# A seven-product second MLP layer whose GpSimd work is handed to VectorE, ScalarE and adding transfers

## The chip, the cores and the metric

The kernel runs on one core of one Trainium2 chip. The metric is the device time of one execution in microseconds (us). Five engines matter: TensorE (PE in the profile, with PEld for its weight loads), VectorE (DVE), ScalarE (ACT), GpSimd (POOL) and the sync engine (SP), which only issues transfers. A transfer can be issued from the queue of SP, of ScalarE or of GpSimd.

## The reference, cut to what matters

One decoder layer on 512 tokens of width 1024. Four branches (sparse attention, gated linear attention, RG-LRU, HGRN2) are merged by gates and projected; then comes the MLP that the change is about:

```python
merged = (gates[:, :, 0] * (y_a @ w_br_a[l]) + gates[:, :, 1] * (y_b @ w_br_b[l])
          + gates[:, :, 2] * (y_c @ w_br_c[l]) + gates[:, :, 3] * (y_d @ w_br_d[l]))
x = x + merged @ w_out[l]
h2 = rms_norm(x, norm2_g[l])
x = x + jnp.square(jax.nn.relu(h2 @ w_ff1[l])) @ w_ff2[l]
return rms_norm(x, final_norm_g)
```

`w_ff1` is 1024x4096 and `w_ff2` 4096x1024, all float32.

## The kernel before

Every matmul operand is split into a high part (a cast to float32r, on ScalarE, L209 for weights) and a low part (operand minus high part, L211, on VectorE, or on GpSimd for weight units 5 to 23). `mm3` (L223 to L229) then issues three matmuls: high by high, high by low, low by high. A weight unit is loaded by SP into a raw buffer, and `split` cuts it into two pieces; the pool `whl` holds four pieces of high and four of low parts.

The stages follow one another on TensorE: input projections with the four branches between them, the gates (32 steps: four branches in the order 2, 0, 3, 1 by eight column blocks `m`, each adding into `merged[m]` on GpSimd, L1052), the output projection, the first MLP layer (`ff1`, 32 units) and the second MLP layer.

The second layer is a 2x2 block product of the hidden activations by `w_ff2`, done in seven products instead of eight (`PRODS`). Product `n` names a left operand (a hidden block `H`, or the difference of two), a right operand (a block of `w_ff2`, or a sum or difference of two, kept in DRAM as `right[...]`) and the output quadrants `(i, j)` into which it is added with a sign. Products 0, 1, 2, 5 and 6 have a difference on the left; products 3 and 4 have a plain block. Each product runs over eight units `g` of twelve matmuls (two pieces by two output strips `t` by three), into two PSUM banks.

What feeds a unit, and what the change touches:
- `make_left(n, g)` makes the left operand: where there is a difference, GpSimd subtracts into a `q` tile (L1195); ScalarE casts the high part (L1204); the low part (L1205) is made by VectorE, or by GpSimd where there was no difference. It is called one product ahead, at the same unit. For product 0 it is called during ff1. `behind` adds ordering without a semaphore; the order on each engine is otherwise set by a planner from the priorities of the bands (`BANDS`: evictions, then weight splits, ..., then `left`, then `mm`).
- `right_unit` loads and splits the right operand, one load on SP and two casts and two subtractions per unit.
- After a product, each of its output strips is evicted by VectorE, `xt += r2 * psum` (L1328): 24 of them, eight of which are the last for their tile `xt[tt, j]` and are followed by a square on ScalarE and, when a row is complete, by `row_out` (final norm and store).
- The right operands that are sums are made in DRAM in 16 pieces of 1 MB: `begin_sum` copies the first block (issued from ScalarE's queue, L1019) and `add_sum` adds the second with an accumulating transfer (issued from GpSimd's queue, L1024). The one that is a difference is made by `difference` (two loads, a GpSimd subtraction L1221, a store L1222) in 16 pieces, during ff1.
- The `q`, `da`, `db`, `sq` and `out` tiles share the tag `y` of NY = 8 buffers. Left operands take twelve places in turn.

## Time and profile before

| | us |
|---|---|
| median of 3 runs | 910.13 |
| lowest, highest | 908.9, 910.93 |
| the profiled execution | 908.9 |
| its span in the trace | 907.1 |
| PE busy | 854.0 (94%) |
| DVE busy | 623.8 (69%) |
| ACT busy | 455.0 (50%) |
| POOL busy | 363.5 (40%) |

Busy time of PE is time with some matmul in flight; a matmul of 512 columns is recorded with 0.39 us but the next one starts before it ends. A row of a timeline gives the start, the length from the first start to the last end, the engine, the line, the operation and how many of them were merged into the row. A row by stretch gives the busy time and the count of instructions of each engine, then the granted clock of TensorE as a share of full speed, the mean busy share of the 16 DMA engines and what they moved.

### The profile page before, as it was taken

What the parts mean: (1) busy time and instruction counts of PE and PEld (TensorE: products, weight loads), DVE (VectorE), ACT (ScalarE), POOL (GpSimd) and SP (SyncE); (2) the same over time, 40 slices, a digit from 0 to 9 for tenths busy, and PEclk for the clock granted to TensorE, in tenths of its full rate; (3) what the DMA queues carried; (4) which work ended last, traced back from release to release, by engine and by line L of the source; (5) the groups of instructions that cost most, each with busy time, mean ns of one, the idle gap of its engine ahead of it and who ended that gap; (6) DMA issues with size and microseconds to landing.
All of it is one profiled execution on the core that took longest, in us unless ns stands there. A gap on an engine that the chain in (4) does not pass through costs nothing.

```text
span 907.1 us, 11859 instructions
## 1 busy us (share of the span) xinstructions
PE 854.0 (94%) x4206; PEld 676.1 (75%) x4206; DVE 623.8 (69%) x1038; ACT 455.0 (50%) x789; POOL 363.5 (40%) x313
## 2 busy tenths in 40 slices
PE   8979978999899999999999999999999969998995
PEld 7757866767677667678888888888888846886674
DVE  8896999797866497966334553434444499769994
ACT  7428664355745673455333443433333345665563
POOL 6345865552432174524222222232222293357500
PEclk9989998999999989999999999999999999999998
DMA  6223212212223245234853598799999646664552
GB/s 242 94 96 105 94 47 87 64 53 76 71 99 110 77 151 186 99 106 164 288 185 106 152 243 202 206 262 270 256 263 258 220 158 196 193 195 140 160 175 83
DMA packets 39083, 141.31 MB, mean 156 GB/s; under 512 B 4683, under 2 KB 6128, under 8 KB 38768
## 3 DMA queue, kind: packets, MB, share of 16 engines
q1 hardware_dynamic: 32880, 102.80, 33.5%
q0 software_dynamic: 5632, 20.97, 11.2%
q10 hardware_dynamic: 512, 16.78, 5.2%
q8 instruction: 33, 0.54, 0.2%
q14 instruction: 26, 0.21, 0.1%
HBM read 134.24 MB, written 40.64 MB: 193 GB/s over the span
## 4 chain that ended last, share of the span: by engine, by line
PE 67%; DVE 23%; issue 4%; ACT 3%; DMA 1%; POOL 1%; SPq 0%; DVEq 0%; POOLq 0%; ACTq 0%
PE m_f L226 6%; PE m_f L225 6%; PE m_f L227 6%; DVE lo L211 6%; PE m_gt L227 5%; PE m_gt L225 5%; PE m_gt L226 5%; PE m_g L226 3%; PE m_g L227 3%; PE m_g L225 3%; PE m_o L225 2%; PE m_o L226 2%; PE m_o L227 2%; PE dal L236 1%; DVE sc L564 1%
## 5 line engine op out<-in xcount | busy, mean ns | idle before, releaser
L209 ACT CAST hi<-raw 128x512 fp32r<-128x512 f32 (+2 forms) x198 | 127.2, 649 | 193.9 <-PE m_f L226 68.2
L211 DVE TENSOR_TENSOR lo<-raw,hi 128x512 fp32r<-128x512 f32 (+2 forms) x160 | 133.3, 837 | 130.7 <-ACT hi L209 128.7
L211 DVE TENSOR_TENSOR lo<-w,hi 128x512 fp32r<-128x512 f32 x112 | 104.0, 947 | 25.8 <-ACT hi L209 25.2
L209 ACT CAST hi<-w 128x512 fp32r<-128x512 f32 x112 | 69.5, 622 | 72.2 <-PE m_g L227 56.7
L227 PE MATMUL m_gt<-hh,lo 128*128 128x512 f32 x256 | 101.5, 397 | 0.0
L226 PE MATMUL m_gt<-hh,hi 128*128 128x512 f32 x256 | 101.5, 396 | 0.0
L225 PE MATMUL m_gt<-hh,hi 128*128 128x512 f32 x256 | 100.8, 394 | 0.0
L225 PE MATMUL m_f<-fh,hi 128*128 128x512 f32 x256 | 99.8, 390 | 0.0
L227 PE MATMUL m_f<-fh,lo 128*128 128x512 f32 x256 | 99.7, 390 | 0.0
L226 PE MATMUL m_f<-fh,hi 128*128 128x512 f32 x256 | 99.6, 390 | 0.0
L1195 POOL TENSOR_TENSOR q<-hd,hd 128x512 f32<-128x512 f32 x40 | 63.5, 1602 | 80.1 <-DVE hd L1237 63.9
L211 POOL TENSOR_TENSOR lo<-raw,hi 128x512 fp32r<-128x512 f32 (+1 forms) x38 | 59.6, 1574 | 45.6 <-ACT hi L209 41.6
L1052 POOL TENSOR_TENSOR mg<-mg,gt 128x512 f32<-128x512 f32 x24 | 41.2, 1719 | 80.5 <-DVE gt L1051 80.5
L226 PEld LDWEIGHTS m_gt<-hh,hi 128*128 128x128 f32 x256 | 48.3, 189 | 11.8 <-issue 1.5
L225 PEld LDWEIGHTS m_gt<-hh,hi 128*128 128x128 f32 x256 | 48.3, 189 | 11.1 <-issue 1.1
L227 PEld LDWEIGHTS m_gt<-hh,lo 128*128 128x128 f32 x256 | 48.2, 188 | 10.9 <-issue 0.3
L227 PEld LDWEIGHTS m_f<-fh,lo 128*128 128x128 f32 x256 | 48.1, 188 | 10.0
L225 PEld LDWEIGHTS m_f<-fh,hi 128*128 128x128 f32 x256 | 48.1, 188 | 9.9
L226 PEld LDWEIGHTS m_f<-fh,hi 128*128 128x128 f32 x256 | 48.1, 188 | 9.8
L1221 POOL TENSOR_TENSOR da<-da,db 128x512 f32<-128x512 f32 x16 | 21.6, 1350 | 63.9 <-DMA db<-in_wts_dram 57.9
L1041 ACT ACTIVATE gt<-m_gt,hbg 128x512 f32<-128x512 f32 x32 | 22.0, 686 | 32.6 <-PE m_gt L227 32.4
L1051 DVE SCALAR_TENSOR_TENSOR gt<-gt,m_br 128x512 f32<-128x512 f32 x24 | 16.4, 684 | 27.0 <-PE m_br L227 26.9
(868 smaller groups left out, 2064.5 us busy)
## 6 DMA issues: line engine op xcount, KB each, us to landing
raw<-in_wts_dram SPq DMA_DIRECT2D x62, 512.0 KB, 4.4
raw<-in_wts_dram SPq DMA_DIRECT2D x32, 640.0 KB, 4.0
w<-right SPq DMA_DIRECT2D x40, 512.0 KB, 4.2
right<-in_wts_dram POOLq DMA_DIRECT2D x16, 1024.0 KB, 9.9
w<-in_wts_dram SPq DMA_DIRECT2D x16, 512.0 KB, 3.5
da<-in_wts_dram SPq DMA_DIRECT2D x16, 256.0 KB, 5.3
db<-in_wts_dram SPq DMA_DIRECT2D x16, 256.0 KB
right<-da POOLq DMA_DIRECT2D x16, 256.0 KB, 9.9
```

Of the source, the lines that this page charges most:

```text
L209: stream["copy"] = S.copy(hi[:, c], raw[:, rc])
L211: stream["lo"] = eng.tensor_sub(lo[:, c], raw[:, rc], hi[:, c].bitcast(F32))
L225: mms = [P.matmul(out, lh, rh, start=start, stop=False), P.matmul(out, lh, rl, start=False, stop=False), P.matmul(out, ll, rh, start=False ...
L226: P.matmul(out, lh, rl, start=False, stop=False),
L227: P.matmul(out, ll, rh, start=False, stop=stop)]
L236: i = P.matmul(*a, **k)
L564: V.match_replace(sc[:, :nk], m8, sc[:, :nk], SENT)
L1041: i_gate[:] = [S.activation(gt, ps, AF.Tanh, scale=0.5, bias=hbg[:, n * 8 + m:n * 8 + m + 1])]
L1051: V.scalar_tensor_tensor(gt, gt, 1.0, ps, op0=OP.add, op1=OP.mult)
L1052: G.tensor_add(merged[m], merged[m], gt)
L1195: G.tensor_sub(t, H[plus, g], H[minus, g])
L1221: i_sub = G.tensor_sub(a, a, b)
```

## The change

- `make_left` is cut into `prepare_left` (the difference, now on VectorE) and `split_left` (the cast on ScalarE and the low part, now always on VectorE). Both run along the units counted through all products: at unit `q` the difference for unit `q + 8` is made, and the split for unit `q + AHEAD`, AHEAD = 6. They are ordered behind the last cast and the last low part of the unit's right operand.
- An eviction that is not the last for its tile is made by ScalarE into a `y` tile (`o`), and an accumulating transfer issued from GpSimd's queue adds it to `xt`. That is 16 of the 24 evictions; the eight last ones stay on VectorE.
- The copies of `begin_sum` are issued at gate steps 2 to 17 (of 32) instead of at two of three steps from 8 on. Eight of the 16 `add_sum` are issued in the last two gate branches (every second step from 16), four stay in the output projection and four are left in ff1, where there were twelve.
- The last 18 matmuls of the last product are held in the written order, which puts the last nine of strip 0 ahead of the last nine of strip 1.

```diff
--- before.py
+++ after.py
@@ -28,6 +28,7 @@
 LEVELS = (32, 16, 8, 4, 2, 1)
 TCARGS = {"schedule_with_timeline_sim": True}
 NPM_BANKS, NA_BANKS, NG_BANKS = 3, 3, 2
+AHEAD = 6
 LAG = 3
 PIECES = 2
 LO0, LO1 = 5, 24
@@ -60,6 +61,9 @@
     ((0, 0), (1, 1), "11-22", ((1, 1, 1), (0, 0, 1))),
     ((0, 1), (1, 1), "21+22", ((0, 0, 1),)),
 )
+
+
+GATES = (2, 0, 3, 1)
 
 
 def gate_units(n):
@@ -1026,7 +1030,6 @@
     merged = [yp.tile([128, T], F32, tag="mg", bufs=KT, name=f"mg{m}") for m in range(KT)]
 
     i_gate = []
-    begun = {"n": 0}
 
     def gates(n, is_first, last):
 
@@ -1035,9 +1038,9 @@
             ps, hi, lo = std_tile(("gate", n, m), f"gt{n}{m}", hh, hl)
             with band("ev"):
                 gt = yp.tile([128, T], F32, tag="gt", bufs=NG, name=f"gt{n}{m}")
-                if not is_first and m % 3 < 2 and begun["n"] < len(pieces):
-                    begin_sum(begun["n"], i_gate)
-                    begun["n"] += 1
+                step = GATES.index(n) * KT + m
+                if 2 <= step < 2 + len(pieces):
+                    begin_sum(step - 2, i_gate or [stream["copy"]])
                 i_gate[:] = [S.activation(gt, ps, AF.Tanh, scale=0.5, bias=hbg[:, n * 8 + m:n * 8 + m + 1])]
             yh, yl = SH[n]
             with band("mm"):
@@ -1049,7 +1052,9 @@
                     V.scalar_tensor_tensor(merged[m], gt, 1.0, ps, op0=OP.add, op1=OP.mult)
                 else:
                     V.scalar_tensor_tensor(gt, gt, 1.0, ps, op0=OP.add, op1=OP.mult)
-                    G.tensor_add(merged[m], merged[m], gt)
+                    i_add = G.tensor_add(merged[m], merged[m], gt)
+                    if step >= 16 and step % 2 == 0:
+                        add_sum((step - 16) // 2, [i_add])
                 if last is not None:
                     dump(f"mg{m}", merged[m])
                     h, l = last(f"mgh{m}", FR), last(f"mgl{m}", FR)
@@ -1151,7 +1156,7 @@
                 S.activation(sq, x2[m], AF.Square)
                 i_acc = G.tensor_add(acc, acc, sq)
                 if m % 2:
-                    add_sum(m // 2, [i_acc])
+                    add_sum(8 + m // 2, [i_acc])
 
 
     xt, r2 = {}, {}
@@ -1185,14 +1190,20 @@
     turns = {"left": 0, "raw": 0}
     H, left = {}, {}
 
-    def make_left(n, g, after=None):
+    def prepare_left(n, g, after=()):
 
         plus, minus = PRODS[n][0:2]
+        t = H[plus, g]
+        if minus is not None:
+            with band("left"):
+                t = yy(f"q{n}{g}")
+                behind([V.tensor_sub(t, H[plus, g], H[minus, g])], after[1:])
+        left[n, g] = t
+
+    def split_left(n, g, after=()):
+
+        t = left[n, g]
         with band("left"):
-            t = H[plus, g]
-            if minus is not None:
-                t = yy(f"q{n}{g}")
-                G.tensor_sub(t, H[plus, g], H[minus, g])
             k = turns["left"] % 12
             turns["left"] += 1
             if k < 8:
@@ -1201,12 +1212,8 @@
             else:
                 h = persist.tile([128, 2, T], FR, tag=f"p{k - 8}", name=f"l{n}{g}")
                 h, l = h[:, 0], h[:, 1]
-            i_h = S.copy(h, t)
-            i_l = (V if minus is not None else G).tensor_sub(l, t, h.bitcast(F32))
-            if after:
-                behind([i_h], after[:1])
-                if minus is not None:
-                    behind([i_l], after[1:])
+            behind([S.copy(h, t)], after[:1])
+            behind([V.tensor_sub(l, t, h.bitcast(F32))], after[1:])
             left[n, g] = h, l
 
     def difference(c):
@@ -1239,11 +1246,12 @@
             if n == 2:
                 turn()
         if j == 1 and kk == 1:
-            make_left(0, g)
+            prepare_left(0, g)
+            split_left(0, g)
         if n % 2 and n // 2 < 16:
             i_sub = difference(n // 2)
-            if n // 2 < 12:
-                add_sum(4 + n // 2, [i_sub])
+            if n // 2 < 4:
+                add_sum(12 + n // 2, [i_sub])
     with band("ev"):
         i_ln = S.preload_act_table_set("natural_log_exp_and_others")
         behind([i_ln], i_gate)
@@ -1301,7 +1309,7 @@
                 SY.dma_start(gf, bass.AP(tensor=gf_in.tensor, offset=gf_in.offset, ap=[[0, 128], [1, D]]))
         with band("mm"):
             pss = [(mbank if n % 2 else abank)(f"m_g{n}{t}") for t in range(2)]
-        blocks = {}
+        blocks, mms = {}, []
 
         order = [(k, t) for k in range(16) for t in range(2)]
         if n == len(PRODS) - 1:
@@ -1313,21 +1321,31 @@
                 for kk in range(2):
                     c = slice(kk * 256, (kk + 1) * 256)
                     blocks[k + kk] = lh[:, c], ll[:, c], hi[kk], lo[kk]
-                if n + 1 < len(PRODS):
-                    make_left(n + 1, k // 2, [stream["copy"], stream["lo"]])
+
+                after = [stream["copy"], stream["lo"]]
+                q = n * 8 + k // 2
+                if q + 8 < len(PRODS) * 8:
+                    prepare_left(*divmod(q + 8, 8), after)
+                if 8 <= q + AHEAD < len(PRODS) * 8:
+                    split_left(*divmod(q + AHEAD, 8), after)
             with band("mm"):
                 lh_, ll_, hi_, lo_ = blocks[k]
                 c = slice(t * 128, (t + 1) * 128)
-                mm3(pss[t], lh_[:, c], ll_[:, c], hi_, lo_, k == 0, k == 15)
+                mms += mm3(pss[t], lh_[:, c], ll_[:, c], hi_, lo_, k == 0, k == 15)
+        if n == len(PRODS) - 1:
+            in_line(mms[-6 * LAG:])
         for i, j, sign in outs:
             todo[i, j] -= 1
         for t in range(2):
             for i, j, sign in outs:
                 tt = 2 * i + t
                 with band("ev"):
+                    if todo[i, j]:
+                        o = yy(f"o{n}{tt}{j}")
+                        S.activation(o, pss[t], AF.Copy, scale=r2[tt, sign])
+                        G.dma_start(xt[tt, j], o, accum_op=OP.add)
+                        continue
                     V.scalar_tensor_tensor(xt[tt, j], pss[t], r2[tt, sign], xt[tt, j], op0=OP.mult, op1=OP.add)
-                    if todo[i, j]:
-                        continue
                     S.activation(yy(f"sq{tt}{j}"), xt[tt, j], AF.Square, accum_out=ssq[:, 2 * tt + j:2 * tt + j + 1])
                     if (i, j) == (0, 1):
                         pre[tt] = {1: yy(f"pre{tt}")}
```

## Rows read from the trace of the kernel before

**Rows 1.** By stretch: busy us (x count) by engine, granted clock, DMA share, GB/s

```profile
160.00:320.00 160.00, 153.74 (x896) 113.87 (x895) 114.62 (x272) 89.52 (x164) 56.82 (x58) 1.00 0.23 78
320.00:400.00 80.00, 76.89 (x492) 59.07 (x490) 64.84 (x105) 41.52 (x64) 43.34 (x41) 0.96 0.42 145
400.00:500.00 100.00, 100.00 (x461) 81.70 (x460) 47.97 (x65) 45.17 (x65) 28.65 (x17) 1.00 0.50 175
500.00:722.00 222.00, 222.00 (x1000) 184.24 (x999) 97.97 (x170) 83.29 (x145) 61.60 (x61) 1.00 0.85 233
722.00:765.00 43.00, 32.98 (x134) 23.94 (x133) 42.14 (x40) 20.67 (x36) 30.04 (x19) 1.00 0.51 174
765.00:822.00 57.00, 57.00 (x253) 47.13 (x252) 42.16 (x54) 36.57 (x62) 21.85 (x16) 1.00 0.65 202
822.00:866.00 44.00, 37.85 (x153) 27.45 (x152) 44.00 (x45) 25.35 (x48) 29.16 (x18) 1.00 0.46 143
866.00:897.00 31.00, 31.00 (x138) 25.54 (x136) 23.09 (x45) 15.68 (x30) 0.00 (x0) 1.00 0.41 136
```

**Rows 2.** Waits from 720 us on: waiter, releaser: total us, times, longest

```profile
PE m_g L226 <- DVE lo L211: 15.9, 13, 2.3
```

**Rows 3.** Timeline of GpSimd in the second layer

```profile
724.08 14.82 POOL L1195 TENSOR_TENSOR q<-hd,hd 128x512 f32<-128x512 f32 x9 [9.63 <-DVE hd L1237]
...
749.09 0.56 POOL L1222 DMA_DIRECT2D right<-da  x1
...
825.69 13.57 POOL L1195 TENSOR_TENSOR q<-hd,hd 128x512 f32<-128x512 f32 x8
```

**Rows 4.** Timeline of VectorE in the second layer: beside GpSimd, and without

```profile
732.64 1.74 DVE L211 TENSOR_TENSOR lo<-w,hi 128x512 fp32r<-128x512 f32 x1
...
761.10 0.68 DVE L1205 TENSOR_TENSOR l21l<-q,l21h 128x512 fp32r<-128x512 f32 x1
...
761.70 1.28 DVE L211 TENSOR_TENSOR lo<-w,hi 128x512 fp32r<-128x512 f32 x2
...
791.74 1.04 DVE L211 TENSOR_TENSOR lo<-w,hi 128x512 fp32r<-128x512 f32 x1 [0.67 <-ACT hi L209]
...
794.46 1.04 DVE L211 TENSOR_TENSOR lo<-w,hi 128x512 fp32r<-128x512 f32 x1 [0.67 <-ACT hi L209]
```

**Rows 5.** Timeline: first matmul of product 0; evictions after products 3 and 6

```profile
722.00 0.39 PE L225 MATMUL m_g<-hi,l00h 128*128 128x512 f32 x1
...
822.29 2.72 DVE L1328 SCALAR_TENSOR_TENSOR xt<-m_g,r,xt 128x512 f32<-128x512 f32 x4
...
896.87 1.41 DVE L1328 SCALAR_TENSOR_TENSOR xt<-m_g,r,xt 128x512 f32<-128x512 f32 x2 [3.68 <-PE m_g L227]
```

**Rows 6.** Timeline of the tail

```profile
896.90 0.39 PE L227 MATMUL m_g<-hi,l67l 128*128 128x512 f32 x1
...
899.77 0.75 DVE L1289 SCALAR_TENSOR_TENSOR out<-xt,fv,gf 128x512 f32<-128x512 f32 x1
...
900.39 0.61 ACT L1331 ACTIVATE sq<-xt 128x512 f32<-128x512 f32 x1
...
902.49 0.75 DVE L1289 SCALAR_TENSOR_TENSOR out<-xt,fv,gf 128x512 f32<-128x512 f32 x1
```

**Rows 7.** Groups of ScalarE, from the page: count, busy us, mean ns

```profile
L209 ACT CAST hi<-w 128x512 fp32r<-128x512 f32 x112 | 69.5, 622 | 72.2 <-PE m_g L227 56.7
...
L1041 ACT ACTIVATE gt<-m_gt,hbg 128x512 f32<-128x512 f32 x32 | 22.0, 686 | 32.6 <-PE m_gt L227 32.4
```

**Rows 8.** Transfers: the queue of GpSimd (page); landing of line 1222 (its own answer)

```profile
q0 software_dynamic: 5632, 20.97, 11.2%
...
DMA to landing us min/median/max: 2.6/9.9/16.0
```

**Rows 9.** Issues by line, of the tensor `right`: ns min/median/max, first and last start

```profile
L1019 ACTq DMA_DIRECT2D right<-in_wts_dram x16: 496/496/604, 241.5 to 471.5; - x16
...
L1024 POOL DMA_DIRECT2D right<-in_wts_dram x16: 860/894/1135, 514.2 to 689.3; - x16
```


## The prediction

> **What bounds the kernel now.** I read the stretches first [rows 1]. From 400 to 722 us TensorE is busy without a gap, 322 of 322 us, so nothing that is added or taken away beside it there moves the end unless it stops TensorE. From 722 us, where the second MLP layer starts, the picture changes twice. In 722 to 765 and in 822 to 866 TensorE is busy for 32.98 of 43 and 37.85 of 44 us, while VectorE is full (42.14 and 44.00 us) and GpSimd is busy for 30 and 29 us. In 765 to 822 and 866 to 897 TensorE is full again and VectorE has room. The waits say who is late: TensorE's low-by-high matmul waits for VectorE's low parts [rows 2]. The granted clock is 1.00 in all of these rows, which is the upper of the two levels, so the clock has no part in it.
>
> The timelines say why VectorE is late. The two stretches are those in which GpSimd makes `q` differences one after another, nine in 14.82 us from 724.08 and eight in 13.57 us from 825.69 [rows 3]. Beside them one low part takes VectorE 1.74 us; without GpSimd the same subtraction takes 0.68, and in a series one starts every 0.60 us (761.10 to 761.70; two in 1.28) [rows 4]. So it isn't the count of VectorE's instructions that stops TensorE but that two engines, each reading two operands, take turns. `make_left` is called at each unit, but nothing holds the GpSimd part back, so the differences of a product bunch at its start.
>
> **The gain at hand.** In the undisturbed part, low parts at the same place of two successive units start at 791.74 and 794.46 [rows 4]: 2.72 us per unit of twelve matmuls. Product 0 starts at 722.00, the evictions after product 3 at 822.29, those after product 6 at 896.87 [rows 5]. Products 0 to 3 took 100.29 us for 32 units that need 32 x 2.72 = 87.04, so 13.25 us are lost; products 4 to 6 took 74.58 us for 24 x 2.72 = 65.28, so 9.30 are lost. Together 22.5 us.
>
> **Part 1, differences to VectorE.** What it removes: the slow turns, and with them the 22.5 us, if VectorE can carry the work. What it adds: per unit VectorE then has two low parts of the right operand, one low part of the left and, for products whose successor has a difference, one difference: 4 x 0.60 = 2.40 us of 2.72 (products 0, 1, 4 and 5), 3 x 0.60 = 1.80 in products 2 and 3, two in most of product 6. It fits, with 0.3 us to spare per unit where it is fullest. It holds only while a subtraction takes 0.60; at 0.68 (its recorded length, were none overlapped with the next) four take 2.72 and nothing is to spare. I take 0.60, since series of that kind stand in the trace. What is queued behind a difference on VectorE is the next unit's low part; it is delayed by at most a difference and a left low part, 1.2 us, while four pieces of right operand are buffered (4 x 1.36 = 5.44 us of matmuls). The GpSimd low parts of products 3 and 4 also move to VectorE; they are counted in the three and four. In ff1 the eight differences of product 0 move too; VectorE is busy for 97.97 of 222 us in 500 to 722 [rows 1], so they cost nothing. One `difference` subtraction and two small products for the final norm stay on GpSimd: at most three times about 1.1 us of delay on VectorE, covered by the same buffer.
>
> **Part 2, evictions to ScalarE and adding transfers.** VectorE loses 16 of 24 evictions at 2.72 / 4 = 0.68 us [rows 5]. ScalarE gains 16. An eviction of it from PSUM with a scale is not in the trace; the nearest row is the gate's tanh, 0.686 us [rows 7]. ScalarE's steady load is three casts, 3 x 0.622 = 1.87 of 2.72 us [rows 7]. After products 0 and 1 it has four evictions in a row, 2.74 us. The piece whose buffer comes free at that moment is needed three pieces later, after 4.08 us: 2.74 + 0.62 for its cast + 0.60 for its low part = 3.96 us. That just holds. If it doesn't, each of these two ends costs some tenths, at most about 1 us; after the other products there are two evictions and over 1 us to spare. I put 1.0 us on the sum for all of this, with 0 and 4 as ends (the upper one: 2 x 1 us here, and 2 us of VectorE catching up at 0.3 us per unit).
>
> The adding transfers are new. The sixteen of 256 KB go to the queue that moved 20.97 MB in 11.2% of sixteen engines' 907 us, 4.84 us per MB [rows 8], so 16 x 0.25 x 4.84 = 19 us of a transfer system whose share is 0.41 to 0.65 in these stretches [rows 1]: some 0.11 more. Who waits for one: the next addition to the same `xt`, one product (21.8 us) later at the earliest, and the reuse of its `y` buffer. After the four evictions of a product the next four units take the other four of eight buffers for their differences; the fifth difference, in VectorE's queue, needs the first `o` again, some 4 x 2.72 = 10.9 us after the evictions, and TensorE feels a stopped VectorE only about 2 us later. So a landing decides from about 12 us on. Line 1222 has the same size and queue: 2.6, 9.9 and 16.0 us as least, median and most [rows 8], the long ones in ff1, where the share is 0.85. In the second layer I expect the lower end, so no cost, with the rival below for the other.
>
> [...] The trace first: at 749.09, in the stretch where VectorE was full, GpSimd's issue took 0.56 us [rows 3]. [...]
>
> **Part 3, the places of the weight sums.** Copies: sixteen issues of 0.50 us on ScalarE's queue [rows 9] move ahead, six of them into branch 2's gates, around 160 to 320 us. There TensorE has gaps, so a delay on ScalarE can count: at most 6 x 0.5 = 3 us. The transfers are at a low there (share 0.23). Additions: twelve of sixteen were in ff1, eight of these move to gate steps 16 to 30, about 400 to 500 us, at 0.89 us of GpSimd each [rows 9]; GpSimd is busy for 28.65 of 100 us there and TensorE has no gap. Each MB is 4.84 us of all engines, so 38.7 us leave ff1 (share 0.85 to about 0.68) and come to a stretch at 0.50, which gives up most of its copies. TensorE had no gap at 0.85 either. So nothing in ff1 and the gates, and 0 for the early part, between -2 (another order of the branches' work, which the planner makes anew) and +3.
>
> **Part 4, the last 18 matmuls in order.** Before, the strips ended side by side: strip 0's eviction starts at 896.87, the last matmul at 896.90 [rows 5, 6]. The final norm of the two rows then ran one after the other: the first output starts at 899.77, the second row's square waits until 900.39, the second output starts at 902.49 and ends at 903.24 [rows 6]. With nine matmuls, 9 x 0.227 = 2.04 us, between the strips, row 0 is done beside them, and row 1 alone needs what row 0 needed: 896.87 to 899.77 + 0.75, 3.65 us, from about 897.1, so 900.75 instead of 903.24. That is 2.5 us less, or 1.8 if its square still waits for the first row's output on ScalarE (0.7). I take 2.1. What must be ready for it, the last low part, comes 1.4 us earlier in the order than it did; the four-piece buffer covers that.
>
> **Sum.** Against the profiled execution, 908.9: - 22.5 + 1.0 + 0 - 2.1 = 885.3. The profiled one is the lowest of the three, 1.2 below their median, so 886.5 for a median. The bounds: all unknowns at their good end (1.0 to 0, early part -2, tail -2.5) give 883.1; at their bad end (4, +3, -1.8) 892.8.
>
> **Rivals.**
> 1. *The additions land late.* VectorE's queue stands still for a `y` buffer. The ends after which differences are still made and `o` tiles stand before them are those of products 0, 3 and 4. At the longest landing of line 1222, 16.0 us, each costs 16 - 12 = 4 us: 886.5 + 12 = 898.5. [...] Against it: the 0.56 us issue, the shortest landing of 2.6, and a share well under that of ff1. Chance 0.10.
> 2. *VectorE becomes the bound, and the kernel is slower.* Its subtractions stay long for another reason than GpSimd's reads. The mechanism decides at 0.68 us for one. At 0.95 us, a value I assume between the 0.68 of a free subtraction and the 1.04 of one that GpSimd delays in part [rows 4], four take 3.80: 32 units x 1.08 = 34.6, and 16 units x 0.13 (three take 2.85) = 2.1, together 36.7 lost instead of 22.5: 886.5 + 36.7 = 923. For it: the plan leaves 0.3 us per unit. Against it: the series at 0.60 ran beside transfers and a full TensorE. Chance 0.03.
> 3. *The change doesn't spread the work.* The planner lets differences and splits bunch before weight low parts as GpSimd's did; at 0.60 us per instruction eight in a row are 4.8 us, close to the buffer; with the left low parts behind them they pass it, and if nearly all of the 22.5 us came back in this way, the time would be about 908. Against it: both are ordered behind the low parts of their own unit, and the splits can't run ahead of their place. Chance 0.03.
> 4. *More than the sum*: the early part falls into a better order, or VectorE's relief also takes waits in 160 to 400 us, where TensorE lacks 9 us: 880. Chance 0.04.
>
> **How the numbers follow.** The forecast (886.5, its own range 883 to 893) has 0.80, rival 1 0.10, rivals 2 and 3 0.03 each, rival 4 0.04. The range takes the forecast's bounds and a little of rivals 1 and 4: 881 to 894. A measurement of this kernel can tell about 0.2% (1.8 us) from no change. Faster: 0.80 + 0.10 + 0.04 = 0.94; half of rival 3 within: 0.02; slower, rival 2 and the rest of rival 3: 0.04.
>
> **What the profile would show.** Right: from product 0 to the last eviction some 153 us instead of 174.9; no wait of TensorE for a low part beyond a few tenths; VectorE's subtractions at 0.60 to 0.69 us all through; VectorE near 88% in products 0, 1, 4 and 5. The two outputs at the end some 2 us apart from the strips' order, the tail shorter by 2. Wrong: a wait of VectorE for a transfer of `xt` (rival 1), subtractions over 0.68 in series without GpSimd (rival 2), bunches of differences ahead of low parts (rival 3), or a start of product 0 away from 722 by more than 3 us (part 3).

## The result, and the profile after

| | before | after |
|---|---|---|
| median of 4 runs, us | 909.61 | 884.54 |
| lowest, highest | 908.9, 910.93 | 883.89, 888.01 |
| the profiled execution, its span | 908.9, 907.1 | 885.11, 883.3 |

Before now has a fourth execution, one more than in the table ahead of the prediction. The ratio of after to before is 0.9731, with a 95% interval of 0.9702 to 0.9759: 2.7% faster, where 886.5 us (881 to 894) was predicted. A second series of the same kernel (z1 below), beside its own runs of before, gave a median of 886.05 and 0.9746 [0.9723, 0.9769]. One execution of run b1 below, of 1193.23 us at a granted clock of 0.65, is left out of all of b1's figures.

The stretches of after, from the same view as [rows 1]: busy us (x count) of PE, PEld, DVE, ACT and POOL, then the granted clock, the DMA share and GB/s.

```profile
400.00:500.00 100.00, 100.00 (x460) 81.99 (x460) 46.00 (x65) 44.97 (x65) 34.32 (x25) 1.00 0.65 159
500.00:722.00 222.00, 222.00 (x1001) 184.23 (x1000) 102.18 (x177) 83.90 (x145) 46.31 (x46) 1.00 0.67 200
722.00:765.00 43.00, 43.00 (x191) 35.58 (x190) 40.98 (x67) 29.46 (x53) 12.86 (x6) 1.00 0.87 262
765.00:822.00 57.00, 56.74 (x250) 46.51 (x250) 44.86 (x68) 41.90 (x75) 10.05 (x10) 1.00 0.81 224
822.00:866.00 44.00, 44.00 (x196) 36.38 (x195) 41.87 (x76) 31.04 (x60) 3.46 (x4) 1.00 0.70 202
```

The holes of TensorE at 722 to 765 and 822 to 866 are gone: 43.00 of 43 us and 191 matmuls where there were 134. VectorE is hardly less busy there, 40.98 and 41.87 us for 42.14 and 44.00; it does 67 instructions in the first stretch where it did 40. ff1 moves less (0.67 for 0.85) and the second layer more (0.87 for 0.51). The waits of TensorE from 720 us on, which were 15.9 us in thirteen places [rows 2], are one, here in the columns waiter, releaser, total us, times, longest:

```profile
PE m_g L230 <- DVE lo L215: 0.3, 1, 0.3
```

The timeline of VectorE shows why. In product 0 its unit is a difference (L1200), a left low part (L1216) and two right low parts (L215), each starting 0.60 us after the one ahead of it:

```profile
729.12 0.68 DVE L1200 TENSOR_TENSOR q<-hd,hd 128x512 f32<-128x512 f32 x1
729.72 0.68 DVE L1216 TENSOR_TENSOR l<-q,l 128x512 fp32r<-128x512 f32 x1
730.32 1.28 DVE L215 TENSOR_TENSOR lo<-w,hi 128x512 fp32r<-128x512 f32 x2
731.53 0.68 DVE L1200 TENSOR_TENSOR q<-hd,hd 128x512 f32<-128x512 f32 x1
```

From 729.12 to 731.53 is one unit: 2.41 us of VectorE, where TensorE needs 2.72 [rows 4]. In before one low part beside GpSimd took 1.74 us [rows 4].

Where the 23.8 us went (spans 907.1 and 883.3) can be cut at two rows of TensorE, the first matmul of product 0 and the last of product 6. In before they start at 722.00 [rows 5] and 896.90 [rows 6]. In the timeline of after:

```profile
721.01 0.39 PE L229 MATMUL m_g<-hi,l00h 128*128 128x512 f32 x1
...
873.97 0.39 PE L231 MATMUL m_g<-hi,l67l 128*128 128x512 f32 x1
```

| piece | before, us | after, us | difference | predicted |
|---|---|---|---|---|
| up to product 0 | 722.00 | 721.01 | -1.0 | 0 |
| product 0 to the last matmul | 174.90 | 152.96 | -21.9 | -22.5 + 1.0 |
| from there to the span's end | 10.20 | 9.33 | -0.9 | -2.1 |

The layer (the middle piece) is now 56 units at 2.72 us, 152.32, and 0.64 us more. The tail (the last piece) is the one that fell short.

### The profile page after: what moved, and what is told of

The parts are those of the page before. It is cut to its first block, busy times and chain, and to the rows that moved or that the text cites. A ratio compares the mean times of both kernels' runs of the same rounds, so it can differ in the third digit from the quotient of the medians.

```text
span 883.3 us, 11898 instructions
## 1 busy us (share of the span) xinstructions
PE 846.7 (96%) x4206; PEld 677.0 (77%) x4206; DVE 605.4 (69%) x1078; ACT 462.9 (52%) x805; POOL 300.0 (34%) x273
## 3 DMA queue, kind: packets, MB, share of 16 engines
q0 software_dynamic: 7936, 25.17, 14.8%
## 4 chain that ended last, share of the span: by engine, by line
PE 75%; DVE 17%; ACT 4%; issue 2%; DMA 1%; POOL 1%; SPq 0%; DVEq 0%; ACTq 0%; POOLq 0%
PE m_f L231 7%; PE m_f L230 7%; PE m_f L229 7%; PE m_g L230 6%; PE m_g L231 6%; PE m_g L229 5%; PE m_gt L231 5%; PE m_gt L230 5%; PE m_gt L229 5%; DVE lo L215 2%; PE m_o L231 2%; PE m_o L230 2%; PE m_o L229 2%; PE lg L240 2%; PE dal L240 1%
## 5 line engine op out<-in xcount | busy, mean ns | idle before, releaser
L215 DVE TENSOR_TENSOR lo<-raw,hi 128x512 fp32r<-128x512 f32 (+2 forms) x160 | 131.9, 828 | 123.6 <-ACT hi L213 121.6
L215 DVE TENSOR_TENSOR lo<-w,hi 128x512 fp32r<-128x512 f32 x112 | 76.9, 703 | 24.4 <-ACT hi L213 21.7
L1228 POOL TENSOR_TENSOR da<-da,db 128x512 f32<-128x512 f32 x16 | 29.5, 1843 | 147.9 <-DMA db<-in_wts_dram 107.5
L215 POOL TENSOR_TENSOR lo<-raw,hi 128x512 fp32r<-128x512 f32 (+1 forms) x38 | 58.9, 1556 | 45.4 <-ACT hi L213 40.8
L229 PEld LDWEIGHTS m_gt<-hh,hi 128*128 128x128 f32 x256 | 48.4, 189 | 11.2 <-issue 1.1
L231 PEld LDWEIGHTS m_gt<-hh,lo 128*128 128x128 f32 x256 | 48.2, 188 | 10.8 <-issue 0.3
L1346 POOL DMA_DIRECT2D xt<-o x16 | 14.2, 1154 | 86.9 <-ACT o L1345 86.9
```

What stands on the lines that cost most here:

```text
L215: stream["lo"] = eng.tensor_sub(lo[:, c], raw[:, rc], hi[:, c].bitcast(F32))
L229: mms = [P.matmul(out, lh, rh, start=start, stop=False), P.matmul(out, lh, rl, start=False, stop=False), P.matmul(out, ll, rh, start=False ...
L231: P.matmul(out, ll, rh, start=False, stop=stop)]
L1228: i_sub = G.tensor_sub(a, a, b)
L1346: G.dma_start(xt[tt, j], o, accum_op=OP.add)
```

## The experiments

The three pieces of that table, read in the same way from each run's trace (first matmul of product 0; from it to the last matmul; from that to the span's end), with the median of each:

| run | up to product 0 | layer | tail | median, us | ratio to before [95%] |
|---|---|---|---|---|---|
| a1, differences back on GpSimd | 722.20 | 177.13 | 9.27 | 908.97 | 1.0011 [1.0001, 1.0022] |
| a2, the same, held by a wait | 721.90 | 163.97 | 9.23 | 897.04 | 0.9886 [0.9871, 0.99] |
| b1, only the engine changed | 720.33 | 162.49 | 10.28 | 895.06 | 0.9873 [0.9851, 0.9896] |
| a3, evictions on VectorE | 723.38 | 155.10 | 9.32 | 887.12 | 0.9778 [0.9758, 0.9797] |
| a4, old places of the sums | 721.66 | 153.75 | 9.39 | 885.85 | 0.9755 [0.9733, 0.9777] |
| a5, last matmuls in free order | 721.01 | 152.95 | 10.24 | 887.24 | 0.977 [0.9751, 0.9788] |
| a6, squares ahead of the outputs | 721.07 | 153.96 | 8.37 | 884.75 | 0.9741 [0.9725, 0.9756] |
| a7, a fifth subtraction | 722.44 | 163.77 | 9.39 | 897.63 | 0.988 [0.9862, 0.9897] |
| z1, after again | 721.42 | 153.91 | 9.37 | 886.05 | 0.9746 [0.9723, 0.9769] |
| z2, a6 again | 721.27 | 153.09 | 8.44 | 884.95 | 0.9743 [0.972, 0.9767] |
| a8, a6 and the weight difference on VectorE | 721.77 | 153.01 | 8.42 | 884.74 | 0.9734 [0.9712, 0.9756] |
| c1, a6 and all early low parts on VectorE | 717.23 | 153.24 | 8.43 | 878.69 | 0.9673 [0.9648, 0.9699] |

How far such a piece can be trusted is in the table itself. a3, a5, a6, a7, z1, z2 and after have the same program up to product 0, and it starts between 721.01 and 723.38 in them. The layer of a4, a5, a6, a8, z1, z2 and after is nearly the same program and takes 152.95 to 153.96, in two groups: 152.95 to 153.09 in four of these traces, 153.75 to 153.96 in a4, a6 and z1. z1 is the same kernel as after, and its extra time stands in one place, between the first matmul of product 0 and the first one with `l14h`, the fifth unit of product 1. In after, then twice in z1:

```profile
753.71 0.61 PE L229 MATMUL m_g<-hi,l14h 128*128 128x512 f32 x2
...
721.42 0.39 PE L229 MATMUL m_g<-hi,l00h 128*128 128x512 f32 x1
...
755.11 0.61 PE L229 MATMUL m_g<-hi,l14h 128*128 128x512 f32 x2
```

After needs 32.70 us from 721.01, twelve units at 2.72 and nothing more, and z1 needs 33.69. So a difference of 1 us between two layers, read from one trace each, doesn't show an effect of an edit. Where z1 loses it is told under part 2. The tail stands to 0.2 us.

### a1: the differences on GpSimd again

The theory is that the two engines' turns cost the 22 us; the rival is that the new order, or the relief of VectorE by the evictions, brought them.

```diff
-                behind([V.tensor_sub(t, H[plus, g], H[minus, g])], after[1:])
+                behind([G.tensor_sub(t, H[plus, g], H[minus, g])], after[1:])
```

> The changed kernel with one thing undone: the differences of the left operands are again subtracted by GpSimd, at the places in the program that the change gave them. Nothing but free buffers holds GpSimd back. Theory (two-operand reads of GpSimd and VectorE take turns): VectorE's subtractions go back to about 1.7 us beside runs of GpSimd, and 10 to 22 us of the 21.7 that the second layer gained are lost: 895 to 907 us. Rival (the gain came from the new order and the split into prepare and split, not from the engine): 884 to 888 us.

Measured: 908.97 us (907.67 to 910.73), above the 895 to 907 expected; the whole gain is gone, and the layer is 2.2 us longer than in before. The stretches, the timeline of GpSimd and that of VectorE:

```profile
722.00:765.00 43.00, 33.48 (x130) 25.66 (x129) 37.59 (x31) 21.17 (x37) 27.79 (x21) 0.92 0.63 198
...
738.00:742.00 4.00, 1.43 (x4) 1.14 (x5) 4.00 (x4) 0.00 (x0) 1.96 (x2) 0.89 0.00 1
742.00:746.00 4.00, 4.00 (x14) 3.16 (x13) 2.71 (x5) 1.76 (x3) 0.00 (x0) 0.68 0.68 257
746.00:750.00 4.00, 4.00 (x19) 3.32 (x18) 3.75 (x5) 2.32 (x4) 1.29 (x1) 1.00 0.40 136
...
724.28 8.09 POOL L1200 TENSOR_TENSOR q<-hd,hd 128x512 f32<-128x512 f32 x5 [8.24 <-DVE hd L1244]
...
736.20 4.92 DVE L215 TENSOR_TENSOR lo<-w,hi 128x512 fp32r<-128x512 f32 x2
```

`behind` is an order for the planner and no wait: nothing holds GpSimd's differences back, so they run one after another as soon as `hd` is there, five in 8.09 us, as nine did in before in 14.82 [rows 3]. Two low parts then take 4.92 us. That it came out longer than before has one visible reason: after TensorE had waited for 4.3 us in one piece, up to 740.57, the granted clock of the next stretch was 0.68, and a full 4 us passed 14 matmuls where the next ones pass 19. It fell twice more, to 0.62 in 762 to 766 and to 0.73 in 838 to 842. In before it stayed at 1.00 in the whole layer [rows 1]. How much of the 2.2 us this makes wasn't measured apart. Evictions on ScalarE, adding transfers, places of the sums and the order of the tail are all still in a1, so none of them, nor all together, brings the gain while GpSimd makes the differences.

### a2: GpSimd makes them, but each must wait for its unit

Is it the engine, or only that the differences bunch? Here each GpSimd difference waits with a semaphore for its unit's last low part.

```diff
-                behind([V.tensor_sub(t, H[plus, g], H[minus, g])], after[1:])
+                i = G.tensor_sub(t, H[plus, g], H[minus, g])
+                for e in after[1:]:
+                    tc.add_manual_dep(i.ins, e.ins.name, mybir.DependencyInfo(mybir.DependencyClass.Sync, ...
```

> As the one before, but each difference on GpSimd waits by a semaphore for the last low part of its unit, so that one difference runs per unit. Theory (taking turns costs by the piece): one difference of GpSimd delays VectorE by about 1.1 us per unit; three subtractions of 0.60 and 1.1 us are 2.9 us of 2.72, so 0.2 us x 32 units = 6 us are lost: 889 to 893 us. Rival (only bunches hurt): 884 to 886 us.

Measured: 897.04 us (896.59 to 898.31), above the 889 to 893 expected; the layer takes 163.97. Half of the loss goes with the bunches, half stays. The timeline of GpSimd and VectorE in product 0:

```profile
742.03 1.68 POOL L1200 TENSOR_TENSOR q<-hd,hd 128x512 f32<-128x512 f32 x1 [1.23 <-DVE lo L215]
744.94 1.68 POOL L1200 TENSOR_TENSOR q<-hd,hd 128x512 f32<-128x512 f32 x1 [1.23 <-DVE lo L215]
...
739.57 2.38 DVE L215 TENSOR_TENSOR lo<-w,hi 128x512 fp32r<-128x512 f32 x2
...
742.48 2.38 DVE L215 TENSOR_TENSOR lo<-w,hi 128x512 fp32r<-128x512 f32 x2
```

One difference per unit makes VectorE's pair 2.38 us instead of 1.28, 1.1 us more. Three subtractions at 0.60 and this 1.1 are 2.9 us, and differences start 2.91 us apart: VectorE is over 2.72 even when the work is spread. That gives 32 x 0.19 = 6.1 us; the layer lost 11.0 against after. Two places for the rest are seen, the start of product 0, where four differences still run in series (6.39 us from 723.98), and the time after product 0, where GpSimd's queue holds the four issues of the additions (3.62 us from 749.47) ahead of the next difference. What each of them costs, and whether they are all, wasn't measured.

### b1: the kernel before with nothing but the engine changed

```diff
-                G.tensor_sub(t, H[plus, g], H[minus, g])
+                V.tensor_sub(t, H[plus, g], H[minus, g])
```

> The kernel before with one word changed: the differences are subtracted by VectorE, nothing else. Theory (the engine is what matters): most of the second layer's loss goes: about 20 of 22.5 us, 888 to 892 us. Rival (the engine alone is not enough: in the old places the differences bunch on VectorE ahead of weight low parts): half or more of the loss stays, 898 to 909 us.

Measured: 895.06 us (894.94 to 897.23); the layer takes 162.49. It lies between what theory and rival gave: 12.4 of the 21.9 us come with the engine alone. The waits of TensorE from 720 us on, and VectorE's timeline in products 4 and 5:

```profile
PE m_g L226 <- DVE lo L211: 5.3, 5, 2.5
...
818.46 3.69 DVE L1195 TENSOR_TENSOR q<-hd,hd 128x512 f32<-128x512 f32 x6
822.07 1.28 DVE L211 TENSOR_TENSOR lo<-w,hi 128x512 fp32r<-128x512 f32 x2
...
841.82 3.70 DVE L1195 TENSOR_TENSOR q<-hd,hd 128x512 f32<-128x512 f32 x6
```

This is rival 3 of the prediction as it looks on VectorE: six differences in a row, 3.69 us, ahead of the low parts of the right operand that TensorE needs. In after none of these runs is longer than two. Nothing in b1's program ties a difference to its unit behind that unit's low parts. The clock adds to it: after the wait of 2.5 us, which ended at 738.27, the granted clock of b1 was 0.63 in 738 to 742, and TensorE passed 10 matmuls in 3.73 busy us, which at 0.227 us each would be 16. That is an estimate of 1.5 us of b1's layer.

### a3: all evictions on VectorE, no adding transfers

```diff
-                    if todo[i, j]:
-                        o = yy(f"o{n}{tt}{j}")
-                        S.activation(o, pss[t], AF.Copy, scale=r2[tt, sign])
-                        G.dma_start(xt[tt, j], o, accum_op=OP.add)
-                        continue
                     V.scalar_tensor_tensor(xt[tt, j], pss[t], r2[tt, sign], xt[tt, j], op0=OP.mult, op1=OP.add)
+                    if todo[i, j]:
+                        continue
```

> The changed kernel with the evictions put back: VectorE adds all 24 from PSUM, no adding transfers. Theory of the prediction (evictions are no part of the gain; VectorE has 0.3 us per unit to spare and a buffer of four pieces): four evictions are 2.7 us in one place, of which at most about 1 us per product end stops TensorE: 884 to 889 us. Rival (VectorE at 88% can't take them): 16 x 0.68 = 10.9 us come back on the path, 891 to 896 us.

Measured: 887.12 us (885.92 to 889.62), as expected; the layer takes 155.10, 2.1 us more than after and 1.2 more than z1. Waits of TensorE, and VectorE's timeline after product 0:

```profile
PE m_g L230 <- DVE lo L215: 1.7, 2, 1.1
...
747.66 2.72 DVE L1343 SCALAR_TENSOR_TENSOR xt<-m_g,r,xt 128x512 f32<-128x512 f32 x4
750.30 0.68 DVE L215 TENSOR_TENSOR lo<-w,hi 128x512 fp32r<-128x512 f32 x1
```

Four evictions hold VectorE for 2.64 us, and with 0.3 us to spare per unit it has no stock to meet that. So part 2 is worth 1.2 to 2.1 us in the traces, and 1.1 to 2.6 by the medians (against 886.05 and 884.54); the size is rough.

With b1 this gives the layer as a chain: 174.90, less 12.4 for the engine (b1), less 7.4 for the order, with the left low parts of products 3 and 4 taken from GpSimd and the new places of the sums (a3), less 2.1 for the evictions (after; 1.2 with z1). The 7.4 contain the 1.5 us that the clock adds in b1. The steps hold in this sequence only: a1 has the order and the evictions, and without the engine they bring nothing.

### a4: the old places of the weight sums

Copies, and additions, are put back where before has them.

```diff
...
-                step = GATES.index(n) * KT + m
-                if 2 <= step < 2 + len(pieces):
-                    begin_sum(step - 2, i_gate or [stream["copy"]])
+                if not is_first and m % 3 < 2 and begun["n"] < len(pieces):
+                    begin_sum(begun["n"], i_gate)
+                    begun["n"] += 1
...
-                    if step >= 16 and step % 2 == 0:
-                        add_sum((step - 16) // 2, [i_add])
...
-                    add_sum(8 + m // 2, [i_acc])
+                    add_sum(m // 2, [i_acc])
...
-            if n // 2 < 4:
-                add_sum(12 + n // 2, [i_sub])
+            if n // 2 < 12:
+                add_sum(4 + n // 2, [i_sub])
```

> The changed kernel with the weight sums at their old places (copies at two of three gate steps from 8 on, twelve of sixteen additions in ff1). Theory of the prediction (the places cost and bring nothing): within 1 us of the changed kernel, 883.5 to 886 us. Rival 1 (the 1.0 us by which the second layer begins sooner in the changed kernel comes from them): 885 to 886 us with the first matmul of product 0 at 722 instead of 721. Rival 2 (the additions in ff1 crowd the transfers that the fuller second layer now needs): a wait for weight loads in product 0 and over 887 us.

Measured: 885.85 us (885.05 to 887.59), as expected; its interval overlaps that of after. By stretch, ff1:

```profile
500.00:722.00 222.00, 222.00 (x1001) 184.25 (x1000) 100.99 (x177) 83.35 (x145) 53.43 (x54) 1.00 0.85 234
```

The transfers go back from a share of 0.67 to one of 0.85, and TensorE has no gap in either. Part 3 changes who moves what when, and nothing of the time that these runs can show. Product 0 starts at 721.66, inside the spread of the others: the 1.0 us by which after starts earlier than before is not the sums' doing.

### a5: the last 18 matmuls in free order

```diff
-        if n == len(PRODS) - 1:
-            in_line(mms[-6 * LAG:])
```

> The changed kernel without the fixed order of the last 18 matmuls. Theory (the order brings what the trace of the changed kernel shows at the tail): 1.1 us slower, 885.6 us, with both last evictions side by side and some 6.1 us from the last matmul to the end of the second output. The prediction's own term: 2.1 us, 886.6. Rival (the order is nearly what the planner would choose anyway): no difference.

Measured: 887.24 us (886.03 to 888.64), above the 885.6 expected. Up to the last matmul the trace is after's (873.96); then the tail is 10.24, which is before's 10.20, instead of 9.33. So part 4 is worth 0.9 us in the trace, and it is the whole of the tail's gain. The medians go the same way, by 2.7 us against after and 1.2 against z1, but their intervals overlap.

### a6 and z2: each row's square ahead of the other row's output

The tail of after was to be 2.1 us shorter than before's and is 0.9. Its timeline:

```profile
872.34 0.75 DVE L1348 SCALAR_TENSOR_TENSOR xt<-m_g,r,xt 128x512 f32<-128x512 f32 x1 [2.08 <-PE m_g L231]
873.12 0.63 ACT L1349 ACTIVATE sq<-xt 128x512 f32<-128x512 f32 x1 [3.59 <-DVE xt L1348]
...
874.40 0.20 ACT L1288 ACTIVATE fv<-fv 128x1 f32<-128x1 f32 x1
874.40 0.75 DVE L1348 SCALAR_TENSOR_TENSOR xt<-m_g,r,xt 128x512 f32<-128x512 f32 x1 [0.36 <-PE m_g L231]
875.07 0.14 DVE L1287 TENSOR_SCALAR fv<-fv 128x1 f32<-128x1 f32 x1
...
875.94 0.72 ACT L1295 ACTIVATE out<-pre,fv 128x512 f32<-128x512 f32 x1 [1.34 <-DVE fv L1291]
876.57 0.61 ACT L1349 ACTIVATE sq<-xt 128x512 f32<-128x512 f32 x1
...
878.67 0.75 DVE L1297 SCALAR_TENSOR_TENSOR out<-xt,fv,gf 128x512 f32<-128x512 f32 x1
```

The first row's square starts 0.78 us after its eviction, the second row's 2.17 us after it (874.40 to 876.57), because it stands behind the first row's output on ScalarE, and this output is late, since the second strip's eviction stands ahead of the first row's small step L1287 on VectorE. To test that, both evictions and squares of a product are written ahead of its `row_out` calls:

```diff
+        done = []
         for t in range(2):
...
                     if todo[i, 0] == 0 and todo[i, 1] == 0:
-                        row_out(tt)
+                        done.append(tt)
+        for tt in done:
+            row_out(tt)
```

> The changed kernel with the final norms of a product's rows written after both of its evictions and squares, so that the second row's square stands ahead of the first row's output on ScalarE. Theory (the missing 1 us of the tail's term is this place in ScalarE's queue): the second square starts right after its eviction, at about 0.8 us instead of 2.2 us, and the time is 1.0 to 1.4 us lower, 883.1 to 883.5 us. Rival (the stores at the end, issued one after another, set the end): under 0.4 us.

> The second square ahead of the first output, once more beside the changed kernel. Theory (in the trace the tail after the last matmul got 1.0 us shorter, and what was lost before it was the run's own): 1.0 us under the changed kernel of this call. Rival (the new order of the rows at the ends of products 4 and 5 costs TensorE what the tail gains): equal to it.

> The changed kernel itself, so that the three below are compared on the same chip: 884 to 885 us. It also tells how far the start of product 0 moves between runs of one program: before product 0 the programs of the earlier runs were alike, and it stood between 721.0 and 723.4 us.

Measured: 884.75 us (883.91 to 885.21) and, again, 884.95 (884.55 to 887.31), where after has 884.54 and, again, 886.05. The first misses the 883.1 to 883.5 expected, the second is 1.1 below z1, as expected, but inside its interval. The timeline of a6:

```profile
875.46 0.75 DVE L1349 SCALAR_TENSOR_TENSOR xt<-m_g,r,xt 128x512 f32<-128x512 f32 x1 [0.36 <-PE m_g L231]
...
876.24 0.63 ACT L1350 ACTIVATE sq<-xt 128x512 f32<-128x512 f32 x1 [0.58 <-DVE xt L1349]
```

The square starts 0.78 us after its eviction, and the tail is 8.37 to 8.44 us in all four kernels with this order, against 9.33 and 9.37 in the two runs of after. That is 0.9 to 1.0 us in every trace, and less than the medians of two such kernels can tell apart: the wait is shown, the gain in time isn't.

### a7: a fifth subtraction per unit

What decides whether VectorE is the bound? Each difference of products 1, 2, 5 and 6 is made twice, with the same values.

```diff
                 behind([V.tensor_sub(t, H[plus, g], H[minus, g])], after[1:])
+                if n:
+                    behind([V.tensor_sub(t, H[plus, g], H[minus, g])], after[1:])
```

> The changed kernel with each difference of products 1, 2, 5 and 6 subtracted twice on VectorE (32 subtractions more, the second overwrites the first with the same values). Theory (VectorE is at four subtractions of 0.60 in 2.72 us, so a fifth passes the bound): in these 32 units one unit takes 5 x 0.60 = 3.01 us, 0.29 x 32 = 9.3 us, less what the buffers take up at the start of each stretch, 2 to 4 us: 890 to 894 us. Rival (there is more slack than the prediction says): 885 to 887 us.

Measured: 897.63 us (895.95 to 898.01), 11.6 to 13.1 above after and above the 890 to 894 expected. The layer is 10.8 us longer than in after, 9.9 longer than in z1. Five at 0.60 are 3.02 us of 2.72, and 32 x 0.30 = 9.6. The buffers do take up the first units: TensorE's first wait for a low part, 0.65 us, ends at 737.31, 14.9 us or some five units into the layer. So nearly the whole excess is paid, and what the buffers saved is lost elsewhere. Two places are seen in VectorE's timeline, where the full engine now waits:

```profile
741.45 0.69 DVE L1200 TENSOR_TENSOR q<-hd,hd 128x512 f32<-128x512 f32 x1 [1.19 <-POOL da L1230]
...
754.63 0.69 DVE L1200 TENSOR_TENSOR q<-hd,hd 128x512 f32<-128x512 f32 x1 [0.44 <-DMA xt<-o]
```

The first is a wait of 1.19 us that ends with GpSimd's `da`, which took 8.93 us from 732.49; the second is the wait of rival 1, for an adding transfer, 0.44 us. Neither stands among VectorE's waits of after.

### a8: the last weight difference on VectorE too

One GpSimd subtraction falls into product 0 of after, `da` of the weight difference. It showed something that I hadn't expected (last section). Here all sixteen of them are moved, on top of a6:

```diff
-            i_sub = G.tensor_sub(a, a, b)
+            i_sub = V.tensor_sub(a, a, b)
```

> As the one before, and the sixteen subtractions of the weight difference are on VectorE too, so that GpSimd has only transfers and two products for the norm in the second MLP layer. Theory (the one GpSimd subtraction in product 0 got its turn only after 8.7 us and then delayed VectorE by 1.1 us, which the buffer covers): equal to the one before within 0.5 us. Rival (it costs TensorE part of what is lost in product 0): up to 1 us faster.

Measured: 884.74 us (883.62 to 885.29), layer and tail as in z2. What GpSimd does once in product 0 costs the kernel nothing.

### c1: the same cure in the early part

If the turns are the cause, then the low parts that GpSimd makes for weight units 5 to 23 cost VectorE's other work in the branches as well. On top of a6:

```diff
-LO0, LO1 = 5, 24
+LO0, LO1 = 5, 5
```

> As the square-first kernel, and the low parts of weight units 5 to 23, which GpSimd makes in the early stages (38 subtractions, 1.56 us each), go to VectorE. Theory (taking turns costs VectorE about 1.1 us for each GpSimd subtraction beside it, doing it itself costs 0.60): 38 x 0.5 = 19 us of VectorE are freed between 60 and 240 us, of which TensorE, which lacks some 13 us there, gets 2 to 6: 878 to 882 us. Rival (in that stretch VectorE has long series and other work, GpSimd's subtractions fall into its gaps): VectorE, at 80 to 90% there, becomes later, 886 to 895 us.

Measured: 878.69 us (877.4 to 881.57), as expected, 6.3 below z2 and faster than both kernels. By stretch, 60 to 160 us of c1, then of z2; and TensorE's longest waits up to 160 us in z2, with the one of c1 that answers to the second:

```profile
60.00:160.00 100.00, 98.11 (x542) 78.20 (x540) 93.09 (x190) 64.98 (x120) 28.98 (x25) 1.00 0.32 105
...
60.00:160.00 100.00, 90.04 (x484) 71.66 (x483) 91.60 (x162) 61.18 (x110) 61.40 (x49) 0.97 0.24 81
...
PE m_c_x L229 <- DVE z_a_q L427: 5.0, 1, 5.0
PE pT L246 <- DVE L L632: 4.2, 1, 4.2
...
PE pT L246 <- DVE L L632: 0.8, 1, 0.8
```

VectorE does 190 instructions in 93.09 us where it did 162 in 91.60, and TensorE is busy for 8 us more. The 5.0 us wait isn't in c1's list at all. The granted clock, 0.97 in z2 and 1.00 in c1, has a part in this. c1 doesn't separate the end of the turns from the plain fact that a low part takes GpSimd 1.56 us in the mean of the 38, and VectorE 0.60 where several stand in a series; for the turns speaks that VectorE does 28 instructions more in 1.5 us more. Not all of it stays: from 0 to 160 us TensorE is busy for 12.3 us more than in z2 (154.11 and 141.83), but product 0 starts only 4.0 us earlier. Between 160 and 320 us c1 passes 818 matmuls where z2 passes 895, after a wait for `yal` (L651) of 4.2 us, which is 0.9 in z2, and with a granted clock of 0.66 in 280 to 300, where z2 has 1.00. The profiled run of c1 is 2.0 us above its median; so 4.0 us are placed by the traces, and the rest of the 6.3 only measured.

## Why the prediction was right, step by step

**The bound, and the 22.5 us.** Right, and tested from both sides: a1 gives the loss back, after has nearly none. The layer fell by 21.9 us, 22.5 less a leftover of 0.6 (in z1 by 21.0, with 1.6 left); the undisturbed pitch of 2.72 us was the right measure of what is lost. The clock of 1.00 "in all of these rows" holds from 400 us on, which is where the argument needs it; 320 to 400 us has 0.96 [rows 1]. The two levels are 1.00 and 0.50 when before is read by half microseconds, and from 328 to 901 us it stands at 1.00.

**Part 1.** Four subtractions at 0.60 us are 2.41 us a unit, against the 2.40 predicted. The margin of 0.3 us is real: a7 spends it and pays after some five units. VectorE is busy for 95% of 722 to 765 instead of the 88% predicted. The forecast counted a unit in its steady state; the stretch also holds the 1.1 us for `da`, and VectorE works ahead without a pause up to 744.15. The prediction gave the turns as the whole cause and the new order as a guard against rival 3. The runs divide it otherwise: the engine alone brings 12.4 us, the order about 7, part of it by the clock.

**Part 2.** The 1.0 us put on the sum is there in some traces and not in others. In after the layer has 0.6 us left over, and none of it is at a row of four evictions; in z1, the same kernel, and in a4 and a6, 0.8 to 1.1 us over twelve units of 2.72 are lost between the first matmul and `l14h`. ScalarE's timeline after product 0 in after, and the casts and evictions of z1:

```profile
742.61 2.42 ACT L1345 ACTIVATE o<-m_g,r 128x512 f32<-128x512 f32 x4 [0.33 <-issue]
744.90 0.63 ACT L213 CAST hi<-w 128x512 fp32r<-128x512 f32 x1
...
742.35 1.14 ACT L213 CAST hi<-w 128x512 fp32r<-128x512 f32 x2 [3.28 <-DMA w<-in_wts_dram]
...
744.44 2.41 ACT L1345 ACTIVATE o<-m_g,r 128x512 f32<-128x512 f32 x4
```

The next cast starts 2.29 us after the first eviction, not the 2.74 assumed from single lengths, for each starts before the one ahead has ended. With 0.62 for the cast and 0.60 for the low part it is 3.5 us of the 4.08 there are. In z1 the casts ahead of the row had waited 3.28 us for a weight load, against 1.42 in after; the row then stands right behind late casts, and the low parts after it come late. That the late load is the cause is read from the two traces and wasn't tested. The length itself was right, 0.682 us against the tanh's 0.686 [rows 7]. What the prediction didn't say is that part 2 carries 1.2 to 2.1 of the 22.5 us (a3): without it VectorE can't keep up after products 0 and 3.

**The adding transfers.** They are off the path, as forecast. The answer of their own line, L1346: issue ns as least, median and most, and the landing.

```profile
L1346 POOL DMA_DIRECT2D xt<-o x16: 856/981/1891, 743.6 to 863.6; - x16
...
DMA to landing us min/median/max: 3.3/4.7/10.3
```

The longest landing, 10.3 us, lies below the 12 at which, by the prediction's estimate, a late one would decide. Their price was too low: the queue's share goes from 11.2% of 907.1 us [rows 8] to 14.8% of 883.3 in the page of after, 29 us for 4.2 MB where 19 were worked out, 7 us per MB instead of 4.84, if its other transfers cost what they did. No wait of VectorE or TensorE in this layer of after is put down to a transfer. ScalarE's casts do wait for weight loads, 3.8 us in three places, but all three (729.29, 731.86 and 740.09) stand ahead of the first addition, at 743.60.

A full VectorE left no mark on the one issue that can be compared: that of the weight difference, L1229, took 0.56 us at 739.68, where VectorE works without a pause, and 0.56 in the median of all sixteen, fifteen of them in ff1, where VectorE is at 46%. The issues of the additions, with VectorE at 79 to 95% (722 to 866 us), took 0.98 in the median, and the additions landed in 4.7.

**Part 3.** Nothing, as forecast (a4), with ff1's share at 0.67 where 0.68 was worked out. The 1.0 us of the early piece is inside the spread of identical programs (2.4 us).

**Part 4, the step that failed.** -2.1 was predicted, -0.9 measured, and a5 gives this 0.9 back. The failed step is that "row 0 is done beside" the nine matmuls of the other strip. They take 2.04 us, and row 0's norm needs 3.65 by the prediction's own rows: it was still running when strip 1 came, so that the two rows met on VectorE and ScalarE. The lower end, 1.8, allowed for one such meeting of 0.7 us; there were two, worth 1.39 (the second square 2.17 us after its eviction instead of 0.78). The other 0.2 us is the start: strip 1's eviction begins 0.43 us after the last matmul's start (873.97 to 874.40), where 0.2 was taken. Together they are the whole distance from the full term, 2.5, to 0.9. With the squares first (a6, z2) the tail is 1.8 us shorter than before's, the prediction's lower end.

**The sum.** For the profiled execution 885.3 was predicted, 885.11 measured. That it is closer than the terms were is luck: the tail was 1.2 us short, the early piece came 1.0 early for no reason that the runs show, the layer was 0.4 better (in z1 0.5 worse). The median, 886.5 predicted, was 884.54 and then 886.05.

**The rivals.** 1: no late landing in after; its wait exists once VectorE is overfull (a7, 0.44 us). 2: the subtractions stayed at 0.60, so it didn't decide; a7 shows that a fuller VectorE does, after some five units. 3: it is what b1 does, and it costs about 7 of 21.9 us rather than nearly all. 4: the early part did hold a gain of the same kind, but this change doesn't take it; c1 does.

## What to carry to other kernels

When VectorE feeds TensorE, price a helper on GpSimd by what it does to VectorE's neighbours, not by its own time: here one GpSimd subtraction beside VectorE's pair of low parts made that pair 1.1 us longer (2.38 us for 1.28, a2), more than the 0.60 that VectorE needs to do it itself. Then look at the order: work made ahead needs an order behind the work that is due now, or it bunches in front of it (about 7 us here, with the clock). And where two results share a tail, compare the distance between them with the length of the tail before counting one as hidden.

## What the runs showed of the hardware that I had not expected

One GpSimd subtraction beside a full VectorE took 8.69 us. In after one `da` falls into product 0. The timeline of GpSimd, and of VectorE where it ends:

```profile
730.70 8.69 POOL L1228 TENSOR_TENSOR da<-da,db 128x512 f32<-128x512 f32 x1 [15.95 <-DMA db<-in_wts_dram]
...
737.55 2.38 DVE L215 TENSOR_TENSOR lo<-w,hi 128x512 fp32r<-128x512 f32 x2
```

Sixteen such subtractions take 1.29 us in the median, this one 8.69. VectorE starts some twelve of its own in that time, at 0.60 us each, before one pair is 1.1 us late. It took 8.70 to 8.96 us in a5, a7, z2 and c1 and 5.31 in b1, but only 2.72 in z1, the same kernel as after, and 1.76 to 3.05 in a3, a4 and a6; in z1 VectorE stood for 0.28 us just then, waiting for a cast (733.50). In before and in a1, where GpSimd had differences queued one behind another, the engines took turns one for one, at about 1.7 us a turn ([rows 3], [rows 4]; VectorE's instructions start 1.67 to 1.70 us apart from 729.24 to 741.04 in before and from 729.45 to 736.20 in a1), and a held difference of a2 took 1.68, as long as one VectorE subtraction of 0.60 and the 1.1 by which VectorE's pair grew. By these turns `da` would have taken about 1.7 us too; some twelve VectorE subtractions started while it ran. Why, and whether it was at work from the start that the profile gives it, is open. It cost nothing here (a8).

The second is the clock: it never left 1.00 in the second layer of before, though TensorE lacked 10 of 43 us there [rows 1], in waits of at most 2.3 us [rows 2]. In a1 it fell to 0.68 in a 4 us stretch (742 to 746) after one wait of 4.3 us, and in b1 to 0.63 (738 to 742) after one of 2.5.
